# Moving the transposed layer input inside SBUF: six distances from a 128-byte boundary, one for each sub-layer

## The chip, the cores and the metric

The kernel runs on one core of a Trainium2 chip. The core has a matrix engine (TensorE, PE in the tables; its weight loads stand in a row of their own, PEld), a vector engine (VectorE, DVE), an engine for activation functions (ScalarE, ACT), GpSimd (POOL), and SyncE (SP), which here issues the DMAs. SBUF is the on-chip memory with 128 partitions; PSUM takes what TensorE produces. The metric is the device time of one launch in microseconds (us); a lower one is better. Each number of the profile comes from one profiled execution. A word is four bytes, the size of one float32.

## The reference

The computation is a decoder trunk of two layers on an input of 256 positions by 1024 features. Each layer has three sub-layers, and each sub-layer begins by normalising its input:

```python
for l in range(DEPTH):                      # DEPTH = 2
    h = h + 0.5 * swiglu(rms_norm(h, ffn1_norm[l]), ffn1_w_in[l], ffn1_w_out[l])
    u = rms_norm(h, mix_norm[l])
    ... = jnp.split(u @ w_in[l], split_points, axis=-1)      # nine parts
    y_s = mamba2_branch(...)                # SSD branch, 2048 wide
    y_d = deltanet_branch(...)              # gated delta rule, 8 heads
    merged = (sigmoid(gate_s) * (y_s @ ssm_w_branch[l])
              + sigmoid(gate_d) * (y_d @ dn_w_branch[l]))
    h = h + merged @ w_out[l]
    h = h + 0.5 * swiglu(rms_norm(h, ffn2_norm[l]), ffn2_w_in[l], ffn2_w_out[l])
return rms_norm(h, final_norm)
```

`swiglu` multiplies by a 1024 x 5632 matrix, forms silu(gate) * up, and multiplies by a 2816 x 1024 matrix. The mixer's `w_in` has 1024 rows and 11,312 columns.

## The kernel before

Every large matrix product is made in split precision. A float32 operand `a` is written as a high part and a low part, both of the type float32r, and the product is the sum of three matmuls: high by high, high by low, low by high (`mm3`, `mm3w`). The weights come from DRAM in tiles of 128 x 1024 (`wraw`, L95), and ScalarE and VectorE split each into `whi` (L60) and `wlo` (L63), some tiles ahead of the matmuls.

A matmul has two operands in SBUF: the stationary one, 128 x 128, which a weight load brings into the array, and the moving one, which streams through it, one column after another. In the profile's rows a matmul of the form `128*128 128x512` has a stationary operand of 128 x 128 and 512 moving columns.

The normalised input of a sub-layer is transposed on TensorE (`hnT`, L184) and split into the two tiles `uTh` and `uTl`. Each has 8 blocks (`KT`) of 256 words in every partition, so 8192 bytes. `rms_chain` writes them (ScalarE the high part, VectorE the low one), and three helpers read them:

- `tok_chunk` has the input as the **stationary** operand and 512 columns of the weights as the moving one (matmuls `f` in the feed-forward sub-layers and `t` in the mixer, L209 to L211).
- `chan_chunk` has 128 columns of the weights as the stationary operand and the 256 positions of the input as the **moving** one (matmuls `fc` in the feed-forward sub-layers, and `kk`, `qq`, `vv`, `zd`, `bc` and `xs` in the mixer, L214 to L216).
- `scalars` in the mixer does the same with 48 columns of weights (`psm`).

The other large products do not read the input: the feed-forward output product (`o`, stationary `gh` and `gl`), the branch products (`b`) and the mixer's output product (`o`, stationary `mh` and `ml`), all with 512 moving columns of the weights, through the same lines L209 to L211.

The order of the sub-layers is `ffn`, `mixer`, `ffn` for each of the two layers. `norm_in` makes the next sub-layer's input and is called once at the start and then by `close`, at the end of every sub-layer but the last: six times in all. Each product of a sub-layer runs in the order in which it is written, for the mixer in the order of the list `ORDER`. The framework places each tile once, at a fixed address, pool by pool and in the order of first use, and rounds a tile up to a multiple of 32 bytes.

In the built program every tile that is an operand of a large matmul starts at a multiple of 128 bytes of its partition, apart from `uTh` and `uTl`: ahead of them lies `mhalf`, one word wide, which takes 32 bytes. So `uTh` is at byte 32,928 and `uTl` at byte 41,120, each 32 bytes or 8 words behind a multiple of 128. The slices that a matmul takes of these tiles are 128 or 256 words apart, so each slice stands at the same distance as its tile.

Of the kernel before, what the change touches and what calls it, by code (L numbers as in the profile page):

```python
# [7 lines left out]
F32 = mybir.dt.float32  # L8
F32R = mybir.dt.float32r
# [7 lines left out]
P = 128  # L17
D = 1024
S = 256
# [3 lines left out]
KT = D // P  # L23
FC = FF // 256
GS = 4
LPW = 48 * 5 + 16 + 1
# [3 lines left out]
NRAW = 5  # L30
NSPL = 5
START = 2

# [10 lines left out]
def trunk_kernel(ctx, tc, x, wst, wsm, norms, lpar, rpar, cst, out):  # L46
    nc = tc.nc
    V, A, G, PE = nc.vector, nc.scalar, nc.gpsimd, nc.tensor

    cpool = ctx.enter_context(tc.tile_pool(name="cpool", bufs=1))  # L50
# [3 lines left out]
    sm = ctx.enter_context(tc.tile_pool(name="sm", bufs=1))  # L54
# [4 lines left out]
    def act(o, i, func=AF.Copy, **kw):  # L59
        return A.activation(out=o, in_=i, func=func, **kw)  # L60
# [4 lines left out]
    def stt(o, a, s, b, op0, op1):  # L65
        return V.scalar_tensor_tensor(out=o, in0=a, scalar=s, in1=b, op0=op0, op1=op1)
# [6 lines left out]
    def f(ap):  # L73
        return ap.bitcast(F32)

    def tmp2(name):
        return s2.tile([P, 512], F32, tag="s2", name=name)

    def trb(name):
        return trp.tile([P, 512], F32, tag="tr", name=name)  # L80
# [25 lines left out]
    def ahead(key, n, fn):  # L106
        while state[key] < min(n, n_halves):
            fn(state[key])
            state[key] += 1

    def take():
        j = state["taken"]
        state["taken"] = j + 1
        ahead("loaded", j + NSPL + NRAW - 1, load)
        ahead("prepped", j + 1 if state["hold"] else j + NSPL, prep)
        return halves.pop(j)
# [28 lines left out]
    LIMT = cs[:, 3 * P + 64 : 4 * P]  # L145
    SEL = [cs[:, 4 * P : 5 * P], cs[:, 5 * P : 6 * P]]
    LAST = cs[:, 6 * P : 7 * P]
    mhalf = cpool.tile([P, 1], F32, name="mhalf")
    V.memset(mhalf[:], -0.5)

    one = cpool.tile([1, P], F32, name="one")
# [5 lines left out]
    Y = [cpool.tile([P, 512], F32, name=f"Y{i}") for i in range(2)]  # L157
    for y in Y:
        G.memset(y[:], 0.0)
    uTh = cpool.tile([P, KT, S], F32R, name="uTh")  # L160
    uTl = cpool.tile([P, KT, S], F32R, name="uTl")

    def rstd_of(t):

# [9 lines left out]
    def rms_chain(t, nw):  # L174
        r = rstd_of(t)
        hns = []
        for n in range(2):
            hn = tmp2("hn")
            ins = stt(hn[:], h[:, t, n * 512 : (n + 1) * 512], r, nw[n], ALU.mult, ALU.mult)
            hns.append(hn)  # L180
        for n in range(2):
            bank = trb("hnT")
            for k in range(4):
                PE.transpose(bank[:, k * P : (k + 1) * P], hns[n][:, k * P : (k + 1) * P], ident)  # L184
            oh = uTh[:, 4 * n : 4 * n + 4, t * P : (t + 1) * P]
            ol = uTl[:, 4 * n : 4 * n + 4, t * P : (t + 1) * P]
            bv = bank[:].rearrange("p (k t) -> p k t", k=4)
            done = [act(oh, bv), tt(ol, bv, f(oh), ALU.subtract)]
        return ins, done

    def norm_in(nw, add=None):

        for t in range(2):
            with tc.high_priority(offset=PRI):
                if add:
                    add(t)
                ins, done = rms_chain(t, nw)
            if t == 0:
                state["hold"] = False
                n = state["taken"]  # L200
                if not add:
                    ahead("prepped", n + 1, prep)
                    with tc.issue_after(done[0].ins), tc.issue_after(done[1].ins):
                        ahead("prepped", n + START, prep)
                with tc.issue_after(ins.ins):
                    ahead("prepped", n + 2, prep)
# [10 lines left out]

    def tok_chunk(ps, ks):

        ws = [(k, take()) for k in ks[::2]]  # L220
        for t in range(2):
            for k0, (wh, wl) in ws:
                for k in range(2):
                    kt = k0 + k
                    mm3(
                        ps[t][:],
                        uTh[:, kt, t * P : (t + 1) * P],
                        uTl[:, kt, t * P : (t + 1) * P],
                        wh[:, k * 512 : (k + 1) * 512],
                        wl[:, k * 512 : (k + 1) * 512],  # L230
                        kt == 0,
                        kt == KT - 1,
                    )

    def chan_chunk(ps):

        ws = [take(), take()]
        for a in range(2):
            for q in range(2):
                wh, wl = ws[q]  # L240
                for k in range(4):
                    kt = 4 * q + k
                    c0 = k * 256 + a * P
                    mm3w(
                        ps[:, a * 256 : (a + 1) * 256],
                        wh[:, c0 : c0 + P],
                        wl[:, c0 : c0 + P],
                        uTh[:, kt, :],
                        uTl[:, kt, :],
                        kt == 0,  # L250
                        kt == KT - 1,
                    )
# [76 lines left out]

    def mixer(l, nxt):  # L330
        with tc.issue_after(state["last"].ins):
            lp = cpool.tile([P, LPW], F32, tag="lp", name="lp")
            nc.sync.dma_start(lp[:], lpar[l])
            rp = cpool.tile([P, RPW], F32, tag="rp", name="rp")
            nc.sync.dma_start(rp[:], rpar[l].partition_broadcast(P))
            wsr = s2.tile([P, KT, 48], F32, tag="s2", name="wsr")
            nc.sync.dma_start(wsr[:], wsm[l])
# [50 lines left out]

        def scalars():
            psm = trb("psm")  # L390
            for kt in range(KT):
                mm3w(psm[0:48, 0:S], wsh[:, kt, :], wsl[:, kt, :], uTh[:, kt, :], uTl[:, kt, :], kt == 0, kt == KT - 1)
            smT = s2.tile([48, S], F32, tag="s2", name="smT")
            act(smT[:], psm[0:48, 0:S])
            pst = trb("pst")
            for t in range(2):
                PE.transpose(pst[:, t * 48 : (t + 1) * 48], smT[:, t * P : (t + 1) * P], ident[0:48, 0:48])
            pv = pst[:, 0:96].rearrange("p (t c) -> p t c", t=2)
            scr = s2.tile([P, 5, 2, 40], F32, tag="s2", name="scr")
            xb, ax, z, s_, q_ = (scr[:, i] for i in range(5))  # L400
            tt(xb, pv[:, :, 0:40], rp[:, None, 0:40].to_broadcast([P, 2, 40]), ALU.add)
            act(dq[:, :, 8:16], pv[:, :, 40:48], AF.Tanh, scale=0.5)
            ts(dq[:, :, 8:16], dq[:, :, 8:16], 0.5, ALU.mult, 0.5, ALU.add)
            ea = small([P, 40], "ea", 1)
            act(ea[:], alog, AF.Exp)
            stt(ax, xb, -1.0, xb, ALU.mult, ALU.max)
            act(z, ax, AF.Exp, scale=-1.0)
            ts(s_, z, 2.0, ALU.add)
            V.reciprocal(out=s_, in_=s_)
            tt(s_, s_, z, ALU.mult)  # L410
            tt(q_, s_, s_, ALU.mult)
            ts(z, q_, 1.0 / 15.0, ALU.mult)
            for d_ in (13.0, 11.0, 9.0, 7.0, 5.0, 3.0):
                stt(z, z, 1.0 / d_, q_, ALU.add, ALU.mult)
            stt(z, z, 1.0, s_, ALU.add, ALU.mult)
            ts(ax, xb, 0.0, ALU.max)
            stt(sp[:], z, 2.0, ax, ALU.mult, ALU.add)
            stt(la[:], sp[:], -1.0, ea[:, None, :].to_broadcast([P, 2, 40]), ALU.mult, ALU.mult)
            yield
            psr = trb("psr")  # L420
            for t in range(2):
                PE.matmul(psr[0:40, t * 256 : (t + 1) * 256], la[:, t, :], UU, start=True, stop=True)
            pr = psr[:].rearrange("p (t c) -> p t c", t=2)
            V.tensor_copy(rows[0:32], pr[0:32, :, 0:P])
            V.tensor_copy(rows[32:40], pr[32:40, :, P : 2 * P])
            nc.sync.dma_start(rdram[:], rows[:].rearrange("p t c -> p (t c)"))
            pac = trb("pac")
            for t in range(2):
                PE.transpose(pac[:, t * 40 : (t + 1) * 40], rows[:, t, :], ident[0:40, 0:40])
            V.tensor_copy(ac[:], pac[:, 0:80].rearrange("p (t c) -> p t c", t=2))  # L430
            V.tensor_copy(dq[:, :, 0:8], ac[:, :, 32:40])
            yield
            psp = trb("psp")
            for c in range(4):
                PE.matmul(psp[:, c * 16 : (c + 1) * 16], SEL[c % 2], dq[:, c // 2, :], start=True, stop=True)
            for a in range(2):
                V.tensor_copy(
                    pq[64 * a : 64 * a + 64].rearrange("p k h c -> p c k h"),
                    psp[64 * a : 64 * a + 64, 0:64].rearrange("p (c k h a) -> p c k h a", c=4, k=2, h=4)[:, :, :, :, a],
                )  # L440
# [709 lines left out]
```

## Time and profile before

| | before |
|---|---|
| median of 3 runs | 1592.82 us (1592.76 to 1594.43) |
| the profiled execution, its own time | 1593.43 us |
| its span, from the first to the last instruction | 1591.6 us |
| TensorE busy | 1572.3 us, 99% of the span |
| VectorE busy | 1069.1 us, 67% |
| ScalarE busy | 880.1 us, 55% |
| granted TensorE clock | 0.999 of full speed |

Of each group of instructions the profile gives the busy time, which is the union of their spans, and the mean span of one. Matmuls are pipelined: one starts while the one before it is still in the array, so the mean span of a matmul is longer than the distance from its start to the next one's start. That distance is called the pitch here. It sets how long a run of matmuls takes, and it is read from the timeline, which gives the start of each instruction in us: the first start, the last start, and the number of steps between them.

### The profile page before, as it was taken

The page shows a single profiled execution, that of the slowest core. Times are in us where ns is not written, and L with a number is a line of the kernel's source. Part 1 is how long each engine was busy: PE and PEld are TensorE (multiplying, and loading weights), DVE is VectorE, ACT ScalarE, POOL GpSimd, SP SyncE. Part 2 cuts the span into 40 slices and gives each one's busy share as a digit, 9 for nine tenths or more (in the row PEclk, how much of TensorE's full clock was granted, in tenths as well). Part 3 has the DMA queues.
Part 4 walks back from the last instruction along what each step waited for, and adds up shares of the span by engine and source line. Part 5 has one row for each costly group of instructions (what it writes and reads, how often), then busy time and mean ns, then how long its engine had stood idle before and what let it go on. Part 6 is the DMA issues. An engine that isn't in the chain of part 4 may idle for free.

```text
span 1591.6 us, 28859 instructions
## 1 busy us (share of the span) xinstructions
PE 1572.3 (99%) x11672; PEld 1420.9 (89%) x11672; DVE 1069.1 (67%) x1550; ACT 880.1 (55%) x1416; POOL 58.1 (4%) x60
## 2 busy tenths in 40 slices
PE   8999999999999999999999999999999999999998
PEld 7999879999888888999899987899998888889986
DVE  5555468957899766555465555698579996675554
ACT  5444468756565654444354444686656665454443
POOL 0000020000000000000000001000000000000000
PEclk9999999999999999999999999999999999999999
DMA  7555465543465456555565565655436555555562
GB/s 268 193 188 195 161 203 192 166 149 117 173 214 172 159 170 189 188 192 190 173 207 190 186 196 174 197 176 180 129 120 207 178 170 175 172 175 194 187 196 96
DMA packets 91915, 284.73 MB, mean 179 GB/s; under 512 B 22069, under 2 KB 23045, under 8 KB 90758
## 3 DMA queue, kind: packets, MB, share of 16 engines
q1 hardware_dynamic: 91782, 282.90, 54.8%
q8 instruction: 91, 1.49, 0.4%
q14 instruction: 42, 0.34, 0.1%
HBM read 280.94 MB, written 1.92 MB: 178 GB/s over the span
## 4 chain that ended last, share of the span: by engine, by line
PE 91%; DVE 4%; DMA 2%; ACT 1%; POOL 1%; issue 0%; SPq 0%; POOLq 0%; ACTq 0%
PE fc L216 9%; PE fc L214 9%; PE fc L215 9%; PE o L211 6%; PE o L209 5%; PE o L210 5%; PE t L209 4%; PE t L210 3%; PE t L211 3%; PE b L211 3%; PE b L210 2%; PE b L209 2%; PE xs L215 2%; PE xs L214 2%; PE xs L216 2%; DVE wlo L63 1%
## 5 line engine op out<-in xcount | busy, mean ns | idle before, releaser
L63 DVE TENSOR_TENSOR wlo<-wraw,whi 128x1024 fp32r<-128x1024 f32 x504 | 613.6, 1223 | 376.4 <-ACT whi L60 369.3
L60 ACT ACTIVATE whi<-wraw 128x1024 fp32r<-128x1024 f32 x504 | 531.0, 1060 | 429.3 <-PE fc L215 176.2
L214 PE MATMUL fc<-uTh,whi 128*128 128x256 f32 x1280 | 357.4, 279 | 0.0
L215 PE MATMUL fc<-uTl,whi 128*128 128x256 f32 x1280 | 357.0, 279 | 0.0
L216 PE MATMUL fc<-uTh,wlo 128*128 128x256 f32 x1280 | 357.0, 279 | 0.0
L215 PEld LDWEIGHTS fc<-uTl,whi 128*128 128x128 f32 x1280 | 240.6, 188 | 0.2
L214 PEld LDWEIGHTS fc<-uTh,whi 128*128 128x128 f32 x1280 | 240.6, 188 | 0.2
L216 PEld LDWEIGHTS fc<-uTh,wlo 128*128 128x128 f32 x1280 | 240.6, 188 | 0.0
L209 PE MATMUL o<-whi,gh 128*128 128x512 f32 x352 | 137.3, 390 | 0.0
L210 PE MATMUL o<-wlo,gh 128*128 128x512 f32 x352 | 137.3, 390 | 0.0
L211 PE MATMUL o<-whi,gl 128*128 128x512 f32 x352 | 137.0, 389 | 0.0
L209 PE MATMUL t<-whi,uTh 128*128 128x512 f32 x256 | 103.2, 404 | 1.0 <-ACT uTh L60 1.0
L210 PE MATMUL t<-wlo,uTh 128*128 128x512 f32 x256 | 101.6, 397 | 0.0
L211 PE MATMUL t<-whi,uTl 128*128 128x512 f32 x256 | 101.1, 396 | 0.0
L211 PEld LDWEIGHTS o<-whi,gl 128*128 128x128 f32 x352 | 66.1, 188 | 13.8
L210 PEld LDWEIGHTS o<-wlo,gh 128*128 128x128 f32 x352 | 66.1, 188 | 13.6
L209 PEld LDWEIGHTS o<-whi,gh 128*128 128x128 f32 x352 | 66.1, 188 | 13.4
L209 PE MATMUL b<-whi,bh 128*128 128x512 f32 x192 | 76.3, 399 | 0.0
L210 PE MATMUL b<-wlo,bh 128*128 128x512 f32 x192 | 74.9, 390 | 0.0
L211 PE MATMUL b<-whi,bl 128*128 128x512 f32 x192 | 74.3, 394 | 0.6 <-DVE bl L63 0.6
L214 PE MATMUL xs<-uTh,whi 128*128 128x256 f32 x256 | 73.1, 286 | 0.0
L216 PE MATMUL xs<-uTh,wlo 128*128 128x256 f32 x256 | 71.6, 280 | 0.0
(259 smaller groups left out, 2915.6 us busy)
## 6 DMA issues: line engine op xcount, KB each, us to landing
wraw<-in_wst_dram SPq DMA_DIRECT2D x504, 512.0 KB, 4.3
dc<-rdram SPq DMA_DIRECT2D x8, 1024.0 KB, 9.2
nw<-in_norms_dram SPq DMA_DIRECT2D x6, 512.0 KB, 4.9
gb<-rdram SPq DMA_DIRECT2D x8, 256.0 KB, 6.1
h<-in_x_dram SPq DMA_DIRECT2D x4, 256.0 KB, 3.1
out_dram<-fo SPq DMA_DIRECT2D x4, 256.0 KB, 2.3
dq<-X SPq DMA_DIRECT2D x2, 256.0 KB, 4.8
cs<-in_cst_dram SPq DMA_DIRECT2D x1, 384.0 KB, 8.2
```

The source lines that it names most:

```text
L60: return A.activation(out=o, in_=i, func=func, **kw)
L63: return V.tensor_tensor(out=o, in0=a, in1=b, op=op)
L209: PE.matmul(ps, lh, rh, start=start, stop=False)
L210: PE.matmul(ps, lh, rl, start=False, stop=False)
L211: PE.matmul(ps, ll, rh, start=False, stop=stop)
L214: PE.matmul(ps, wh, mh, start=start, stop=False)
L215: PE.matmul(ps, wh, ml, start=False, stop=False)
L216: PE.matmul(ps, wl, mh, start=False, stop=stop)
```

## The change

The two tiles of the input become 32 words longer, and start at a multiple of 128 bytes. Each sub-layer uses a view of them that begins some words behind the start: the feed-forward sub-layer that opens layer 0 uses 16, the mixer 24, the second feed-forward sub-layer 4; in layer 1 the three use 12, 20 and 28.

For the start at a multiple of 128 bytes, `mhalf` moves to another pool (`sm`), and so that the tiles behind the input keep their place relative to 128 bytes, the tile `lp` is padded from 257 to 272 words; the DMA still writes 257. In the built program `uTh` is now at byte 32,896 and `uTl` at byte 41,216; the tiles behind `lp` all lie 256 bytes further on, and so at the same distance from a multiple of 128 as before, up to the pool `sm` at the end, whose small tiles move by 288 bytes, or 8 words relative to 128 bytes. The tiles `Y`, `nw`, `lp` and `one` move from 8 words to 0. The instructions of every engine, their order and their waits are the same in both programs.

```diff
+PLACES = (16, 24, 4, 12, 20, 28)
...
-    mhalf = cpool.tile([P, 1], F32, name="mhalf")
+    mhalf = sm.tile([P, 1], F32, name="mhalf", bufs=1)
...
-    uTh = cpool.tile([P, KT, S], F32R, name="uTh")
-    uTl = cpool.tile([P, KT, S], F32R, name="uTl")
+    uT = [cpool.tile([P, KT * S + 32], F32R, name=name) for name in ("uTh", "uTl")]
+    place = {"n": 0}
+
+    def input_at(w):
+
+        return [u[:, w : w + KT * S].rearrange("p (k t) -> p k t", k=KT) for u in uT]
...
-            oh = uTh[:, 4 * n : 4 * n + 4, t * P : (t + 1) * P]
-            ol = uTl[:, 4 * n : 4 * n + 4, t * P : (t + 1) * P]
+            oh, ol = (u[:, 4 * n : 4 * n + 4, t * P : (t + 1) * P] for u in place["u"])
...
     def norm_in(nw, add=None):
 
+        place["u"] = input_at(PLACES[place["n"]])
+        place["n"] += 1
...
     def tok_chunk(ps, ks):
 
+        uTh, uTl = place["u"]
...
     def chan_chunk(ps):
 
+        uTh, uTl = place["u"]
...
-            lp = cpool.tile([P, LPW], F32, tag="lp", name="lp")
-            nc.sync.dma_start(lp[:], lpar[l])
+            lp = cpool.tile([P, 272], F32, tag="lp", name="lp")
+            nc.sync.dma_start(lp[:, 0:LPW], lpar[l])
...
         def scalars():
             psm = trb("psm")
+            uTh, uTl = place["u"]
```

## The prediction

> **What bounds the kernel now.** I read the page first: the engines' busy time, the granted clock, the chain that ended last.
>
> ```profile
> span 1591.6 us, 28859 instructions
> PE 1572.3 (99%) x11672; PEld 1420.9 (89%) x11672; DVE 1069.1 (67%) x1550; ACT 880.1 (55%) x1416; POOL 58.1 (4%) x60
> ...
> PEclk9999999999999999999999999999999999999999
> ...
> PE 91%; DVE 4%; DMA 2%; ACT 1%; POOL 1%; issue 0%; SPq 0%; POOLq 0%; ACTq 0%
> ```
>
> TensorE is busy for 1572.3 of 1591.6 us at the full clock, and 91% of the chain is its own. It has no time in which to wait, so the only thing that a move of its operands can alter is how fast it runs. A busy PE does not say how fast: for that I take the groups by shape, and then the pitch from the timeline. The groups that read the input, and the one that does the same work without it (`o`), are these:
>
> ```profile
> L214 PE MATMUL fc<-uTh,whi 128*128 128x256 f32 x1280 | 357.4, 279 | 0.0
> L215 PE MATMUL fc<-uTl,whi 128*128 128x256 f32 x1280 | 357.0, 279 | 0.0
> L216 PE MATMUL fc<-uTh,wlo 128*128 128x256 f32 x1280 | 357.0, 279 | 0.0
> L209 PE MATMUL o<-whi,gh 128*128 128x512 f32 x352 | 137.3, 390 | 0.0
> ...
> L209 PE MATMUL t<-whi,uTh 128*128 128x512 f32 x256 | 103.2, 404 | 1.0 <-ACT uTh L60 1.0
> L210 PE MATMUL t<-wlo,uTh 128*128 128x512 f32 x256 | 101.6, 397 | 0.0
> L211 PE MATMUL t<-whi,uTl 128*128 128x512 f32 x256 | 101.1, 396 | 0.0
> ...
> L214 PE MATMUL xs<-uTh,whi 128*128 128x256 f32 x256 | 73.1, 286 | 0.0
> ...
> L215 PE MATMUL bc<-uTl,whi 128*128 128x256 f32 x128 | 36.7, 286 | 0.0
> ...
> L216 PE MATMUL qq<-uTh,wlo 128*128 128x256 f32 x128 | 35.7, 279 | 0.0
> L209 PE MATMUL f<-whi,uTh 128*128 128x512 f32 x64 | 26.5, 416 | 1.3 <-ACT uTh L60 1.3
> ...
> L214 PE MATMUL psm<-uTh,wsh 128*48 128x256 f32 x16 | 4.5, 279 | 0.0
> ```
>
> The input is the moving operand of `fc` (3 x 1280), of `xs` (three rows of 256), of `bc`, `zd`, `qq`, `vv` and `kk` (15 rows of 128, the first and the last shown) and of `psm` (three rows of 16): 3840 + 768 + 1920 + 48 = 6576 matmuls of 256 columns. It is the stationary operand of `t` (768) and `f` (three rows of 64, 192): 960 matmuls of 512 columns. The rows already show a difference: `t` and `o` are the same product, yet one `t` takes 396 to 404 ns and one `o` 390.
>
> The timeline gives the pitches. First `fc`, with the input moving at 8 words behind 128 bytes and the weights at 0:
>
> ```profile
> 59.78 0.28 PE L214 MATMUL fc<-uTh,whi 128*128 128x256 f32 x1
> ...
> 64.22 0.28 PE L216 MATMUL fc<-uTh,wlo 128*128 128x256 f32 x1
> ```
>
> 38 steps in 4.44 us, 116.8 ns each. Then `o`, where both operands are at 0:
>
> ```profile
> 159.98 0.39 PE L209 MATMUL o<-whi,gh 128*128 128x512 f32 x1
> ...
> 165.42 0.39 PE L209 MATMUL o<-whi,gh 128*128 128x512 f32 x1
> ```
>
> 24 steps in 5.44 us, 226.7 ns. Last `t`, with the weights moving at 0 and the stationary input at 8 words:
>
> ```profile
> 448.01 0.40 PE L209 MATMUL t<-whi,uTh 128*128 128x512 f32 x1
> ...
> 458.51 0.40 PE L209 MATMUL t<-whi,uTh 128*128 128x512 f32 x1
> ```
>
> 45 steps in 10.50 us, 233.3 ns. No wait lies inside the three stretches. So **8 words of distance go with 6.6 ns more per matmul of 512 columns** (233.3 less 226.7). Per column, `fc` (116.8 for 256, 233.6 for 512) runs at the pace of `t`, and not at the pace of `o`.
>
> **The change part by part.** No instruction, wait or DMA is added, taken away or moved on any queue; what changes are addresses. By distance: each of the four feed-forward sub-layers has 3840 / 4 = 960 moving and 192 / 4 = 48 stationary uses, each of the two mixers (768 + 1920 + 48) / 2 = 1368 and 768 / 2 = 384.
>
> *Distances 4, 12, 20 and 28* (three feed-forward sub-layers and one mixer) are odd multiples of 4 words. Moving: 3 x 960 + 1368 = 4248. Stationary: 3 x 48 + 384 = 528. In the trace of before the operands of these matmuls stand at multiples of 8 words, so no row shows such a distance. Bounds for one moving use: below, the pace without any loss that distance brings; the nearest row is half an `o`, 113.4 ns, a gain of 3.4 ns; a further one is what the second 256 columns of `o` cost over `fc`, 226.7 - 116.8 = 109.9 ns, a gain of 6.9 ns. Above, the whole 6.6 ns of the step from `o` to `t` on each matmul. I take +3.3 ns, which is that step scaled from 512 to 256 columns: the new positions are a finer misplacement than the one that costs 6.6 ns per 512, and I price it as one more such step. 4248 x 3.3 ns = 14.0 us. For a stationary use I take one more step of 6.6 ns, with bounds of -6.6 (the pace of `o`) and +13.2: 528 x 6.6 ns = 3.5 us.
>
> *Distances 16 and 24* (one feed-forward sub-layer, one mixer) are multiples of 8, as before: 2328 moving and 432 stationary uses. I take nothing. The bounds are the same: -3.4 ns (or -6.9) and +6.6 per moving use, -6.6 and +6.6 per stationary one.
>
> The rule that speaks against this sum is in the Trainium skill, "SBUF — State Buffer", section "Specifications (TRN2)": SBUF has lines of 16 bytes, and what costs is a crossing to a new line. All six distances, 0 and 8 too, are multiples of 16 bytes, so by that rule none needs an extra line, and the time would not change. The step from `o` to `t` is between two such distances and measures 6.6 ns, so the trace shows a dependence that the rule does not give.
>
> *What lies beside.* The path of TensorE has little slack for the sum to disappear in. In the six stretches in which the input is read:
>
> ```profile
> 25.00:137.50 112.50, 112.50 (x966) 112.46 (x965) 62.70 (x71) 54.08 (x70) 0.00 (x0) 1.00 0.61 195
> 199.10:589.00 389.90, 386.94 (x3139) 344.61 (x3138) 307.54 (x523) 249.01 (x464) 23.80 (x21) 1.00 0.53 172
> 626.60:739.00 112.40, 112.40 (x965) 112.40 (x964) 62.60 (x71) 54.05 (x70) 0.00 (x0) 1.00 0.60 195
> 813.10:925.50 112.40, 112.40 (x965) 112.40 (x964) 62.61 (x71) 54.05 (x70) 0.00 (x0) 1.00 0.59 195
> 987.10:1375.00 387.90, 386.87 (x3140) 344.58 (x3139) 307.61 (x524) 248.78 (x464) 23.80 (x21) 1.00 0.54 173
> 1412.50:1525.00 112.50, 112.50 (x966) 112.50 (x965) 62.72 (x71) 54.05 (x70) 0.00 (x0) 1.00 0.61 195
> ```
>
> The columns are the window's length and then busy time and count of PE, PEld, DVE, ACT and POOL, the clock, and the share and GB/s of the DMAs. In the feed-forward stretches PE is busy throughout and VectorE for 62.7 of 112.5 us: a slower TensorE lengthens them by its whole loss, and a faster one is not held up. In the mixers PE is idle for 3.0 and 1.0 us, so at most that much of a loss could be hidden; VectorE at 307.5 of 389.9 us could hold a gain back.
>
> *The writes of the input* move too:
>
> ```profile
> L60 ACT ACTIVATE uTh<-hnT 128x512 fp32r<-128x512 f32 x24 | 14.0, 595 | 13.2 <-PE hnT L184 12.0
> ...
> L63 DVE TENSOR_TENSOR uTl<-hnT,uTh 128x512 fp32r<-128x512 f32 x24 | 15.7, 686 | 5.8 <-ACT uTh L60 5.7
> ...
> lp<-in_lpar_dram SPq DMA_DIRECT2D x2, 128.5 KB, 6.0
> ```
>
> 24 of each, mostly behind the matmuls of the product that is ending. I cost them at nothing; uncovered, a tenth more on both kinds would be 3.0 us, with as much for a gain. `mhalf` in another pool and the padded `lp` (two loads of the same bytes, ahead of their use) cost nothing; if the loads were uncovered and a tenth longer it would be 1.2 us.
>
> Sum: 14.0 + 3.5 = 17.5 us on the profiled execution's own 1593.43 us, 1610.9. The median before is 0.6 us lower, so I predict 1610.
>
> The Trainium skill ("TensorE: Matmul & The Clock Gate", section "Step-by-step: what each phase is for") says that weight loads have an SBUF read port of their own and take nothing from the running matmul. By that the stationary distance is free and the sum is 14.0 us; `t` against `o`, where only the stationary input's distance differs, disagrees by 6.6 ns.
>
> **The rivals.** *No effect of these distances.* The fast pace of `o` could be special to 0, with every other distance at the common pace of `t` and `fc`. For it: both run at one pace per column though one has the input stationary and the other moving. Then only noise is left, 1593. The Trainium skill's rule of 16-byte lines (the section named above) ends at the same time.
>
> *Faster.* At some distances the moving stream and the weight load could fall into step as they do in `o`. If only 16 and 24, the coarser ones, do: 2328 x 3.4 + 432 x 6.6 ns = 10.8 us, 1582. If all six do: 6576 x 3.4 + 960 x 6.6 ns = 28.7 us, 1564. For it: `o` does get 226.7 ns. Against it: `fc` already has one operand at 0 and does not reach that pace. It decides as soon as its gain on 2328 uses exceeds the loss on 4248, that is, if the odd distances lose under 10.8 us / 4248 = 2.5 ns per moving use and nothing on the stationary side.
>
> *Dearer.* The odd distances could cost the full 6.6 ns per moving use: 4248 x 6.6 + 528 x 6.6 ns = 31.5 us, 1625; with 16 and 24 like them, 6576 x 6.6 + 960 x 6.6 ns = 49.7 us, 1643. For it: a loss may fall on each matmul, whatever its columns. Against it: `fc` and `t` agree per column.
>
> **How the numbers follow.** Chances: the forecast 0.40, with its own range from 1600 to 1618 (half of the moving price, and one and a half times it); dearer 0.15; no effect 0.17; faster at 16 and 24 0.18, at all six 0.10. The range from 1582 to 1640 leaves out the gain at all six and the top of the dearer case. Within 0.2% (3.2 us, about what can be told from no change) is the case of no effect, 0.17; faster 0.28; slower 0.55.
>
> **What would show it.** The stretches can be laid side by side, since the order is the same. Right: `fc` at 116.8 ns in the first feed-forward sub-layer (16) and near 120 in the other three (4, 12, 28), so 112.5 us there and about 115.7 after; the mixer of layer 0 (24) as before, that of layer 1 (20) about 7 us longer, with `t` near 240 ns. Wrong: pitches that differ among 4, 12, 20 and 28 as much as between them and 16, or an `fc` below 116. `o` must stay at 226.7 everywhere; if it moves, something other than the distance has changed.

## The result

| | before | changed |
|---|---|---|
| median, 4 runs each | 1593.62 us (1592.76 to 1594.56) | 1600.93 us (1600.20 to 1605.15) |
| ratio changed to before, of the means | | 1.0051, 95% interval 1.0032 to 1.0070 |
| the profiled execution, its own time | 1593.43 us | 1605.15 us |
| its span | 1591.6 us | 1603.3 us |
| its granted TensorE clock | 0.999 of full speed | 0.998 |

The change costs 7.3 us of the medians (8.2 us of the means). The changed kernel's profiled execution is the slowest of its four, 4.2 us above their median; the account below says where its extra time lies. The page of the changed kernel:

```profile
span 1603.3 us, 28859 instructions
...
PE 1579.5 (99%) x11672; PEld 1429.6 (89%) x11672; DVE 1069.7 (67%) x1550; ACT 881.7 (55%) x1416; POOL 57.9 (4%) x60
```

The count of instructions is the same, and so are VectorE's and ScalarE's busy times within 2 us; TensorE is busy 7.2 us longer.

To read the pitch of a whole sub-layer in one row I use the view of busy time by window, for the tile `fc` alone. Each row is one feed-forward sub-layer, 90 us long, in which TensorE runs one `fc` after the other. A matmul lasts 0.28 us, so 2.4 of those counted were already running when the window opened: the pitch is 90.00 us / (count - 2.4). Before:

```profile
40.00:130.00 90.00, 90.00 (x773) 90.00 (x773) 6.69 (x16) 5.87 (x16) 1.00 0.59 190
640.00:730.00 90.00, 90.00 (x774) 90.00 (x773) 6.62 (x16) 5.86 (x16) 1.00 0.58 188
830.00:920.00 90.00, 90.00 (x774) 90.00 (x773) 6.61 (x16) 5.86 (x16) 1.00 0.57 188
1430.00:1520.00 90.00, 90.00 (x774) 90.00 (x773) 6.62 (x16) 5.86 (x16) 1.00 0.58 188
```

773 or 774 in each, 116.7 ns. The changed kernel, with 16, 4, 12 and 28 words:

```profile
40.00:130.00 90.00, 90.00 (x772) 90.00 (x771) 6.63 (x16) 5.85 (x16) 1.00 0.57 188
645.00:735.00 90.00, 90.00 (x767) 90.00 (x766) 6.64 (x16) 5.63 (x16) 1.00 0.57 188
835.00:925.00 90.00, 90.00 (x767) 90.00 (x766) 6.64 (x16) 5.88 (x16) 1.00 0.57 186
1440.00:1530.00 90.00, 90.00 (x766) 90.00 (x765) 6.63 (x16) 5.84 (x16) 1.00 0.56 186
```

772 at 16 words, 767, 767 and 766 at the odd multiples of 4. The pitches in the rest of this text are the mean distance from one start to the next over all matmuls of the kind in a sub-layer, without the few gaps above 150 ns (260 for 512 columns). By that measure these four are 117.07, 117.78, 117.78 and 117.77 ns, against 116.68 before in all four.

The mixers, from the timeline. The longest stretch of 256-column matmuls without a break, in the first mixer before:

```profile
241.13 0.28 PE L215 MATMUL kk<-uTl,whi 128*128 128x256 f32 x1
...
268.90 0.28 PE L216 MATMUL kk<-uTh,wlo 128*128 128x256 f32 x1
```

238 steps in 27.77 us, 116.7 ns. The same stretch in the changed kernel, at 24 words and then at 20, and a stretch of `t` in each mixer:

```profile
241.53 0.28 PE L221 MATMUL kk<-uTl,whi 128*128 128x256 f32 x1
...
269.74 0.28 PE L222 MATMUL kk<-uTh,wlo 128*128 128x256 f32 x1
...
452.94 0.39 PE L215 MATMUL t<-whi,uTh 128*128 128x512 f32 x1
...
463.91 0.39 PE L217 MATMUL t<-whi,uTl 128*128 128x512 f32 x1
...
1035.76 0.28 PE L221 MATMUL kk<-uTl,whi 128*128 128x256 f32 x1
...
1063.79 0.28 PE L222 MATMUL kk<-uTh,wlo 128*128 128x256 f32 x1
...
1244.58 0.39 PE L215 MATMUL t<-whi,uTh 128*128 128x512 f32 x1
...
1255.49 0.39 PE L217 MATMUL t<-whi,uTl 128*128 128x512 f32 x1
```

238 steps in 28.21 us (118.5 ns) at 24 words, and in 28.03 us (117.8) at 20. 47 steps of `t` in 10.97 us (233.4 ns) and in 10.91 us (232.1). Over all of a mixer the 256-column pitch is 118.47 at 24 words and 117.89 at 20, where the kernel before had 116.81 and 116.85; `t` is 232.7 and 232.1, where it had 233.2.

So where the time went, as count by difference in pitch: the four feed-forward sub-layers 960 x (0.39 + 1.10 + 1.10 + 1.09) ns = 3.5 us, the mixers 1344 x (1.66 + 1.04) ns = 3.6 us, the stationary uses a gain of 1.0 us. That is 6.1 us of the 11.7 by which the two spans differ. The other 5.6 us are mostly pauses of TensorE in the mixers. Waits of TensorE before:

```profile
PE hnT L184 <- DVE hn L66: 4.3, 8, 1.1
...
PE cbb L778 <- DVE vb L63: 2.0, 2, 1.6
```

and after:

```profile
PE cbb L787 <- DVE vb L64: 6.1, 2, 3.3
PE hnT L189 <- DVE hn L67: 4.9, 9, 1.3
```

The wait at the end of the recurrence (`cbb`) is 4.1 us longer in this execution. The sum of its waits is 6.1 us there against 2.0, and 3.5 in the kernel of the first experiment and 3.7 in a faster one below, so it does not follow the pitch, and its length here is at least in part that of this execution. The medians differ by 7.3 us, nearer to the 6.1 of the pitches.

### The profile page after: what moved, and what is told of

Read it like the earlier page. It is cut to its first block, busy times and chain, and to the rows that moved or that the text cites. A ratio compares the mean times of both kernels' runs of the same rounds, so it can differ in the third digit from the quotient of the medians.

```text
span 1603.3 us, 28859 instructions
## 1 busy us (share of the span) xinstructions
PE 1579.5 (99%) x11672; PEld 1429.6 (89%) x11672; DVE 1069.7 (67%) x1550; ACT 881.7 (55%) x1416; POOL 57.9 (4%) x60
## 4 chain that ended last, share of the span: by engine, by line
PE 91%; DVE 4%; DMA 2%; ACT 2%; POOL 1%; issue 0%; SPq 0%; POOLq 0%; ACTq 0%
PE fc L220 9%; PE fc L221 9%; PE fc L222 9%; PE o L217 5%; PE o L215 5%; PE o L216 5%; PE t L215 4%; PE t L217 3%; PE t L216 3%; PE b L217 3%; PE b L216 2%; PE b L215 2%; PE xs L220 2%; PE xs L221 2%; PE xs L222 2%; DMA dc<-rdram 1%
```

## The experiments

Theory A is the prediction's: the distance behind a multiple of 128 bytes sets the pitch. Its first rival, B, is that other addresses that moved do it. "Place" below is the distance of the high part in words; the "room" is what lies between the end of the high part and the start of the low part. The kernel before had place 8 and no room; the changed kernel has 32 words of room, because each tile became 32 words longer.

### The same distance as before in the changed layout, and other distances in it

`e1_all8`, against the changed kernel:

```diff
-PLACES = (16, 24, 4, 12, 20, 28)
+PLACES = (8, 8, 8, 8, 8, 8)
```

> The changed layout (longer tiles, mhalf and lp moved) with all six sub-layers at 8 words, the distance of before. Theory A, the distance alone sets the pitch: fc 116.7 ns, the mixer's 256-column matmuls 116.8, t 233.2, and the time of before, 1593.6 us within 2. Rival B, the other moved addresses cost it (uTl 128 bytes further from uTh, the tiles behind 256 bytes further on, the small tiles by 8 words): the pitches of the changed kernel, 117.1 to 118.5 ns, and about 1601 us.

Measured: 1605.04 us against 1596.38 for the kernel before on the same chip, ratio 1.0058 (1.0042 to 1.0073). In the view by window, tile `fc`:

```profile
40.00:130.00 90.00, 90.00 (x767) 90.00 (x766) 6.63 (x16) 5.80 (x16) 1.00 0.58 186
645.00:735.00 90.00, 90.00 (x762) 90.00 (x761) 6.65 (x16) 5.84 (x16) 1.00 0.57 185
835.00:925.00 90.00, 90.00 (x762) 90.00 (x761) 6.63 (x16) 5.85 (x16) 1.00 0.59 186
```

767 and then 762 where the kernel before had 774: 117.8 and 118.5 ns, the mixers 118.3, `t` 232.1 to 232.4. The high part is at the very byte at which it was before, and the pitch is another. Theory A falls: one of the other addresses matters. The first sub-layer and the later ones differ by 0.7 ns at one and the same place, which no run explains.

`e2_all0`, the same with `PLACES = (0, 0, 0, 0, 0, 0)`:

> All six at 0 words, a multiple of 128 bytes, like every other operand of a large matmul. Theory A1, both operands at 0 is what gives o its 226.7 ns: t goes to 226.7 and fc to about half, 113.4 ns, so 28.7 us less than before, about 1565 us. Rival A2, the fast pace of o needs a stationary operand at 0 but the moving 256 columns keep a common pace: t 226.7, fc 116.7, about 1587 us. Rival A3, a moving operand at 0 loses as at 16, 24 and the odd distances: fc 117.1 to 118.5 ns and 1590 to 1600 us.

Measured: 1601.6 us against 1596.38, ratio 1.0026 (1.0013 to 1.0039). `fc` is 117.78 ns in all four, the mixers 117.8, `t` 231.4. A1 and A2 fall; A3 gave the range of the pitch, not its reason. The time is above its range, in a comparison in which the kernel before was slower too.

`e3_swap`, the same with `PLACES = (24, 16, 20, 0, 4, 8)`:

> The six sub-layers at 24, 16, 20, 0, 4 and 8 words: the mixers get what feed-forward sub-layers had and the other way round. Theory A, the pitch belongs to the distance: fc 118.5 ns in the first (24), 117.8 to 117.9 in the third (20), 116.7 in the last (8); the mixers' 256-column matmuls 117.1 (16) and 117.8 (4). Rival C, the mixers are slower in themselves at any distance but 8: the mixers 117.9 to 118.5 ns again, and the feed-forward sub-layers 117.1 to 117.8.

Measured (one run, 1605.25 us): `fc` 118.5 ns at 24, 117.8 at 20 and at 0; the mixers 117.7 at 16 and 117.85 at 4. 24 words are slow in either kind of sub-layer, so rival C falls. Theory A misses twice more: the last, 8 words, is at 118.5 and not at 116.7, and 16 words have 117.7 in the mixer where the first sub-layer of the changed kernel had 117.1.

`e4_fine`, the same with `PLACES = (1, 6, 2, 3, 7, 5)`:

> The six sub-layers at 1, 6, 2, 3, 7 and 5 words, no multiple of 4 among them. Theory D, memory is fetched in pieces of 4 words (16 bytes), and a matmul that starts inside a piece needs one more: a step above the 117.8 ns of distance 4 in every sub-layer, of 1.7 to 3.3 ns (4 words of 256 columns at 109.9 ns are 1.7), so fc 119.5 to 121 ns and some 1610 to 1620 us. Theory E, pieces of 8 words: the same as 4 words, fc about 117.8 ns and 1600 us. Rival F, no pieces, the pitch drifts with the distance: fc between 116.7 and 117.8 ns.

Measured (one run, 1613.17 us): 122.2 ns at 1, 121.5 at 2, 117.5 at 3, 120.0 at 5; in the mixers 120.9 at 6 and 117.65 at 7. None of the three theories holds: 3 and 7 cost no more than 4, 1 costs 4.4 ns more. The time lies in theory D's range, but not for D's reason: a rule by pieces of 16 bytes would have made all six dearer than 4 words.

### The room between the two parts, and the place of what lies behind

Both kernels put the two parts in one tile, with a place and a room for each sub-layer. `f1_gap`:

```diff
-    uT = [cpool.tile([P, KT * S + 32], F32R, name=name) for name in ("uTh", "uTl")]
+    uT = cpool.tile([P, WORDS], F32R, name="uT")
...
-        return [u[:, w : w + KT * S].rearrange("p (k t) -> p k t", k=KT) for u in uT]
+        return [uT[:, i : i + KT * S].rearrange("p (k t) -> p k t", k=KT) for i in (w[0], w[0] + KT * S + w[1])]
...
+PLACES = ((8, 0), (8, 0), (8, 32), (8, 64), (8, 32), (0, 0))
+WORDS = 4224
```

> Both parts of the input in one tile, with the distance of the high part and the room between the parts chosen for each sub-layer; the weights stay as many bytes behind a multiple of 512 as before. In the order of the sub-layers, high part at 8, 8, 8, 8, 8, 0 words, and the low part 8192 bytes further on plus 0, 0, 128, 256, 128, 0 bytes. Before it was 8 and 0. Theory B1, the 128 bytes more between the two parts cost: fc 116.7 ns in the first sub-layer, the first mixer 116.8; the third (128 bytes) 118.5 and the second mixer 118.3 as in the run with all at 8. Theory B2, the shift of the weights by 256 bytes costs: fc 116.7 ns and the mixers 116.8 in all with 8 words. Under A, the distance alone, already fallen for 8 words: fc 118.5 ns. For the last, 0 words with 0 bytes between, A says 117.8 ns again.

`f2_gap_far` has `WORDS = 4288`, and everything behind the input 256 bytes further on:

> The same six places of the input, with the weights and everything behind the input 256 bytes further on than in the kernel with the same places (the place of the weights in the changed kernel). Theory B1 (room between the two parts): the same pitches as there, 116.7 ns in the first sub-layer and 118.5 in the third. Theory B2 (shift of the weights by 256 bytes): 118.5 ns in both, and in the mixers 118.3.

One run each, 1604.21 and 1599.91 us, with 1599.41 in a single run of the kernel before. The view by window of `f1_gap`, tile `fc`: 8 words without room, with 32 words of room, with 64, and 0 words without room:

```profile
40.00:130.00 90.00, 90.00 (x774) 90.00 (x773) 6.74 (x17) 5.87 (x16) 1.00 0.59 188
645.00:735.00 90.00, 90.00 (x767) 90.00 (x766) 6.62 (x16) 5.86 (x16) 1.00 0.59 187
835.00:925.00 90.00, 90.00 (x773) 90.00 (x773) 6.62 (x16) 5.87 (x16) 1.00 0.59 188
1440.00:1530.00 90.00, 90.00 (x752) 90.00 (x751) 6.62 (x16) 5.46 (x15) 1.00 0.58 187
```

774, 767, 773 and 752. The second of these sub-layers in `f2_gap_far`:

```profile
645.00:735.00 90.00, 90.00 (x762) 90.00 (x761) 6.61 (x16) 5.63 (x16) 1.00 0.59 187
```

With no room the pitch of before is back, 116.67 ns, and so it is with 64 words (116.68); 32 words cost 1.1 ns in `f1_gap` and 1.8 in `f2_gap_far` (118.5), the same two values that `e1_all8` had in different sub-layers of one kernel. In every other sub-layer the two agree, `fc` with 116.68, 116.68 and 119.99, so 256 bytes more between the input and the weights change nothing without room. B1 holds and B2 falls. The surprise is the last row: at 0 words with no room `fc` takes 120.0 ns in nearly every step, 3.3 more than at 8, while the stationary `f` drops to 227.8, the pace of `o`. With 32 words of room the same place had 117.78 (`e2_all0`). Theory A's value for it falls again.

`h3_gaps` asks for other rooms: `PLACES = ((8, 8), (8, 64), (8, 16), (8, 24), (0, 64), (8, 48))`, `WORDS = 4224`.

> The weights at 0 again. The high part at 8, 8, 8, 8, 0 and 8 words; between the parts 8192 bytes plus 8, 64, 16, 24, 64 and 48 words. Theory P, the room between the parts counts by its remainder to 64 words (256 bytes): the mixers (64 words) as with none, 116.8 ns at 8 words and 120.0 at 0. The others are open; if any room that is no multiple of 64 words costs as 32 did, fc is 117.8 to 118.5 ns in all four feed-forward sub-layers; if the room only puts the low part at another distance, fc lies between the pitches of the two distances.

Measured (one run, 1601.74 us): `fc` 117.8 ns with 8, 16 and 24 words of room, 118.5 with 48; the mixers with 64 words of room 116.8 at place 8 and 119.9 at place 0, as with none. Theory P holds: the room counts by its remainder to 256 bytes. Any other room that was tried costs 1.1 to 1.8 ns at place 8. That the room only puts the low part at another place does not hold for all of them: 32 and 48 words put it at 40 and 56, whose pitches without room are 117.4 and 118.3 (table at the end), and `fc` lies above both ends with 117.8 to 118.5 and 118.5.

### The changed kernel's distances without the room

`h1_near`: `PLACES = ((16, 0), (24, 0), (4, 0), (12, 0), (20, 0), (28, 0))`, `WORDS = 4224`.

> The six distances of the changed kernel, 16, 24, 4, 12, 20 and 28 words, with the two parts of the input 8192 bytes apart as before, not 8320. Theory G, the 128 bytes more between the parts are the whole loss: fc 116.7 ns and the mixers 116.8 at all six, the time of before within 3 us. Rival H, the distance matters too when the parts are 8192 bytes apart, as 0 words did (120.0 ns): pitches that leave 116.7 by 0.5 to 3.3 ns at some of the six, and a time that follows from them, up to 22 us over before if all were at 120.

Measured: 1602.7 us against 1594.9, ratio 1.0050 (1.0036 to 1.0064), the same loss as with the room. But its parts are others. In the view by window, tile `fc`, at 16, 4, 12 and 28 words:

```profile
40.00:130.00 90.00, 90.00 (x766) 90.00 (x766) 6.38 (x16) 5.83 (x16) 1.00 0.58 186
645.00:735.00 90.00, 90.00 (x774) 90.00 (x773) 6.84 (x17) 5.88 (x16) 1.00 0.60 188
835.00:925.00 90.00, 90.00 (x763) 90.00 (x762) 6.61 (x16) 5.86 (x16) 1.00 0.59 185
1440.00:1530.00 90.00, 90.00 (x796) 90.00 (x795) 6.64 (x16) 5.98 (x17) 1.00 0.61 194
```

766, 774, 763 and 796: 117.8, 116.8, 118.3 and **113.5 ns**. The mixers are at 119.9 (24) and 119.1 (20). Summed over the counts, the feed-forward sub-layers gain 0.4 us and the mixers lose 1344 x (3.11 + 2.24) ns = 7.2 us. Theory G falls, rival H holds: without the room the distance matters more, not less, and at 28 words it is a gain.

`h4_fine_near` tries further places: `PLACES = ((32, 0), (1, 0), (2, 0), (40, 0), (3, 0), (6, 0))`.

> Parts 8192 bytes apart, at 32, 1, 2, 40, 3 and 6 words. Theory Q, the place counts by its remainder to 32 words: fc 120.0 ns at 32 as at 0, and 116.7 at 40 as at 8. Rival T, by its remainder to 64 words: other values at 32 and 40. At 1, 2, 3 and 6 words: with pieces of 4 words a matmul that starts inside one needs one more, and its pitch is above that of 0 or 4 words by 1.7 to 3.3 ns; without pieces it is not above 120.0.

Measured (one run, 1607.80 us): `fc` 118.7 ns at 32, 117.65 at 2, 117.4 at 40, 120.0 at 6; the mixers 123.2 at 1 and 117.5 at 3. Theory Q falls and T holds: 32 is not like 0 (120.0) and 40 not like 8 (116.7), so the period is not 128 bytes, on which the change is built. Again 3 words cost little and 1 word the most, so no theory of pieces is borne out.

### The weights moved instead of the input

`h2_weights8` moves every tile behind `rp` by 8 words, the weights among them:

```diff
-            rp = cpool.tile([P, RPW], F32, tag="rp", name="rp")
-            nc.sync.dma_start(rp[:], rpar[l].partition_broadcast(P))
+            rp = cpool.tile([P, RPW + 8], F32, tag="rp", name="rp")
+            nc.sync.dma_start(rp[:, 0:RPW], rpar[l].partition_broadcast(P))
...
+PLACES = ((8, 0), (8, 0), (16, 0), (0, 0), (16, 0), (8, 32))
+WORDS = 4224
```

> The weights, and all tiles of large operands behind them, moved by 8 words (32 bytes), so gh and the weights are both at 8 in o. The input, parts 8192 bytes apart: 8, 8, 16, 0, 16 words, and in the last sub-layer 8 with 128 bytes more between the parts. Theory R, what counts is the place of the input relative to the weights: at 8 words fc 120.0 ns and f 227.8 (as 0 had with the weights at 0), at 16 words fc 116.7, f and t 233; o unchanged at 226.8. Rival S, the input's own place behind 128 or 256 bytes counts: fc 116.7 ns at 8 and 120.0 at 0 words as before, t 233 at 8, and o would leave 226.8.

One run, 1603.61 us. The view by window, tile `fc`, at 8, 16, 0 words, and 8 with room:

```profile
40.00:130.00 90.00, 90.00 (x752) 90.00 (x752) 6.20 (x15) 5.50 (x16) 1.00 0.57 185
645.00:735.00 90.00, 90.00 (x774) 90.00 (x773) 6.57 (x16) 6.08 (x17) 1.00 0.59 188
835.00:925.00 90.00, 90.00 (x762) 90.00 (x762) 6.61 (x16) 5.80 (x16) 1.00 0.58 185
1440.00:1530.00 90.00, 90.00 (x767) 90.00 (x766) 6.61 (x16) 5.84 (x16) 1.00 0.59 188
```

752 at 8 words, 774 at 16: 119.99 and 116.68 ns, the two values that 0 and 8 words had with the weights at 0. `f` follows, 227.85 at 8 words; `t` is 227.7 at 8 and 233.2 at 16. `o`, whose two operands moved together, stays at 226.8. Theory R holds in each of these, S falls: **the place of the input relative to the weights sets the pitch**. In `fc` the weights are only the stationary operand, and the input lies at the byte at which it was in `f1_gap`; so the pitch of the moving stream depends on where the stationary operand lies. The writing of the weights, which moved with them, is not the reason: in the steps in which neither VectorE nor ScalarE runs, 132 and 141 of the first sub-layer's, `fc` has 116.7 ns in `f1_gap` and 120.0 in `h2_weights8`. (The tile that the DMA writes moved too; in `w1_low8`, below, it keeps its place, and the pitch changes all the same.) The Trainium skill ("TensorE: Matmul & The Clock Gate", section "Step-by-step: what each phase is for") gives the two operands read ports of their own and says that loading the next weights takes no read bandwidth from the running matmul. Here the place of the weights is worth 3.3 ns of each matmul, and the measurement decides.

`w1_low8` moves the low weights alone, by 8 words, against `f1_gap`:

```diff
-        lo = wpool.tile([P, 1024], F32R, tag="wlo", name="wlo", bufs=NSPL)
+        lo = wpool.tile([P, 1024 + 64], F32R, tag="wlo", name="wlo", bufs=NSPL)[:, 8:1032]
...
+PLACES = ((8, 0), (8, 0), (28, 0), (48, 0), (28, 0), (0, 0))
+WORDS = 4160
```

> Only the low parts of the weights lie 8 words further, the high parts at 0; the input's parts 8192 bytes apart, at 8, 8, 28, 48, 28 and 0 words. In fc the weights are stationary alone: L221 (high by low input) runs while the low weights of L222 are loaded, the other two while high weights are. Theory W, a matmul's pitch is set by its moving operand's place against the weights that are loaded beside it: only L221 of each three sees another place, so the mean leaves 116.7, 113.5 and 113.4 by about a third of the step that all three make when all weights move (at 8 words 3.3 ns, so 117.8). Rival X, the weights of a matmul itself: L222 changes instead, with the same mean. Rival Y, the weights do not count and the run with all of them moved had another reason: fc 116.7 at 8, 113.5 at 28, 113.4 at 48, 120.0 at 0 words as before.

Measured (one run, 1609.91 us): `fc` 117.74 ns at 8, 117.8 at 28, 118.85 at 48, 118.3 at 0; the mixers 117.7 and 117.8. Rival Y falls. The third of the step that W and X both give is met at 8 words (117.7) alone. By the table at the end the thirds at 28, 48 and 0 words are +1.9, +1.3 and -0.6 ns; measured are +4.3, +5.5 and -1.7. W and X are not told apart: at 28 words all three matmuls of a group leave the 113 to 114 ns that they had, for 116.9, 117.9 and 118.7, so a change in one of them moves the others too. `o`, which streams high and low weights in turn past a stationary operand that did not move, rises from 226.8 to between 231.7 and 233.3. So the pace of a sequence depends on the places of all its operands. It is not simply fast where the weights agree: at 0 words it was slower with both parts of them in line (120.0).

### A version that is faster than both

`b1_all28`: `PLACES = ((28, 0),) * 6`, `WORDS = 4224`.

> All six sub-layers at 28 words, the two parts 8192 bytes apart. Theory R, the place of the input relative to the weights sets the pitch, whatever the sub-layer: fc 113.5 ns in all four feed-forward sub-layers as in the one that had 28 words, 4 x 960 x 3.2 ns = 12.3 us less; the mixers' 2736 matmuls of 256 columns at 113.5 too, 9.0 us less; together about 21 us less than before, some 1574 us. Rival U, 113.5 ns came from that one sub-layer's start or from its place at the end: the others at 116.7 to 120 ns and a time of 1590 to 1605 us. Between the two, the mixers keep 117 to 120 ns and only the feed-forward part gains: 1580 to 1590 us.

Measured: 1579.00 us against 1596.14 for the kernel before on the same chip, ratio 0.9898 (0.9880 to 0.9915). The view by window, tile `fc`:

```profile
40.00:130.00 90.00, 90.00 (x796) 90.00 (x796) 6.61 (x16) 6.12 (x17) 1.00 0.61 195
630.00:720.00 90.00, 90.00 (x796) 90.00 (x795) 6.61 (x16) 5.79 (x16) 1.00 0.61 195
820.00:910.00 90.00, 90.00 (x796) 90.00 (x795) 6.61 (x16) 6.05 (x17) 1.00 0.61 194
1420.00:1510.00 90.00, 90.00 (x797) 90.00 (x796) 7.02 (x17) 5.79 (x16) 1.00 0.61 196
```

796 or 797 in every row: 113.5 ns, half of an `o`. The mixers are at 114.1, `t` still at 233.4. 960 x 4 x 3.2 ns + 1344 x 2 x 2.75 ns = 19.7 us; 17.1 arrive. In the profiled executions TensorE is busy 19.0 us less (1553.3 us) and idle 4.3 us more. Theory R holds, U falls.

`s1_scan` looks for other places: `PLACES = ((36, 0), (52, 0), (44, 0), (60, 0), (60, 0), (48, 0))`.

> Parts 8192 bytes apart, at 36, 52, 44, 60, 60 and 48 words. By theory T, remainders to 64 words (256 bytes) count, these are six new places. If the place relative to the weights counts by its size alone, on either side alike, 36 words (28 less than 64) gives fc 113.5 ns, 60 gives 116.8 as 4, 52 and 44 give 118.3 and 119.1 as 12 and 20, 48 gives 117.8 as 16. If not, the pitches lie anywhere from 113.4 to 120 ns, and a place as good as 28 is one with a locked pattern of 113 and 114.

Measured (one run, 1601.76 us): `fc` 118.7 ns at 36, 119.25 at 44, 117.15 at 60, **113.4 at 48**; the mixers 119.1 at 52 and 117.2 at 60. The place does not count by its size alone: 36 is far from 28 and 48 far from 16. At 48 `f` is 229.5, 3.8 ns less than at 28, and at 60 `f` and `t` are at 227.5 and 228.0, as fast as at 0.

`b2_all48`: `PLACES = ((48, 0),) * 6`, `WORDS = 4224`.

> All six sub-layers at 48 words, parts 8192 bytes apart. Theory R, the place relative to the weights sets both pitches: fc 113.4 ns, the mixers' 256-column matmuls near 114, and t near 229.5 as f had at 48, where 28 words had 233.4. Against the kernel with all at 28, 960 x 3.7 ns = 3.6 us less, about 1575.5 us. Rival V, the stationary pitch does not follow the place in the mixers: t at 233 and 1579 us.

Measured: 1577.64 us against 1596.00, ratio 0.9889 (0.9873 to 0.9906). `fc` is 113.4 to 113.6 ns and `t` 229.2, so theory R holds for the stationary uses too; but the mixers' 256-column matmuls are at 115.3, 1.2 above those at 28. The two versions' intervals overlap.

## Why the prediction was wrong

The direction was right and the size was not: +17.5 us were forecast (1610), +7.3 measured (1600.93), under half. The time lies inside the range from 1582 to 1640, and at the lower end of the forecast's own range from 1600 to 1618; half of the moving price, which that end is said to be, gives 1603. The direction was luck in part: of the 7.1 us that the moving uses lose, 2.6 are at 16 and 24 words, priced at nothing, and all of them were measured with a room between the two parts that the sum does not have.

1. *What bounds the kernel* was right. TensorE's pitch is what the change moved: of 11.7 us between the spans, 6.1 are pitches, and most of the rest is a wait whose length differs between kernels without following the pitch. The writes of the input, `mhalf` and `lp` cost nothing that a row shows. `o` stays at 226.7 to 226.9 ns in every feed-forward sub-layer of the changed kernel.

2. *"Distances 4, 12, 20 and 28"* is the step that failed: the term for the moving uses. It took the 6.6 ns from `o` to `t`, scaled to +3.3 ns for a moving use, and 14.0 us. Measured: +1.0 to +1.1 ns in each, 4.6 us. The 6.6 ns were no price of a misplaced line which a finer misplacement pays again. They were the difference between two places of the input relative to the weights (`t` at place 0 has 227.7 ns, at place 8 233.2), and say nothing of a third place. That `fc` came out alike at 4, 12 and 28, as the prediction asked, is owed to the room: without it these places have 116.8, 118.3 and 113.5 ns.

3. The stationary uses at these distances were given +6.6 ns and 3.5 us; they measure -3.1 to +0.2 ns. Here the sign failed, and with 16 and 24 the stationary uses gain 1.0 us. The kernel before already stood at one of the dearest places, 233.2 ns; 234.1 is the highest seen in a mixer.

4. *"Distances 16 and 24"* were given nothing because they are multiples of 8 words. At 24 the mixer pays 1.66 ns, 2.2 us, the dearest of the six.

5. The premise of all three, that the distance behind 128 bytes is the variable, fell. The period is 256 bytes (`h4_fine_near` rules out 128; `h3_gaps` and `f2_gap_far` find 256), the reference is the weights (`h2_weights8`), and the second variable, the room of 128 bytes that the longer tiles put between the two parts, is not in the sum at all. At 8 words the layout with it costs 8.7 us of the medians (`e1_all8`), and the changes in pitch there come to 9.3 us. In this change it evens things out: with it, the six distances cost 0.4 to 1.7 ns; without it (`h1_near`), from -3.2 to +3.1.

6. Of the rivals, *faster* described a gain that exists, and priced it rightly at half of an `o`: 113.4 ns was forecast for it and 113.5 is what 28 words give. It named 16 and 24, or all six, as the places, and the places are 28 and 48, with no room. Its reason, that the streams fall into step, is not shown: regular steps occur at slow places too (last section). *No effect* falls. The Trainium skill ("SBUF — State Buffer", section "Specifications (TRN2)") gives SBUF lines of 16 bytes and a penalty for each crossing to a new line. That rule does not give what was seen here: places that are all multiples of 16 bytes run from 113.4 to 120.0 ns. *Dearer* was not seen at a multiple of 4 words.

What stays open: which weight load a matmul meets (`w1_low8` did not decide), how the places 28 and 48 come out best, and why one place with one room can have two pitches (117.8 and 118.5 ns at 8 words with 32 of room). No rule that was tried gives the order of the places.

## What to carry to other kernels

Where TensorE is the bound, read the pitch of each group of matmuls from the starts in the timeline and compare groups of one shape: `fc` at 116.7 ns where half of an `o` is 113.4 was the trace of a placement that cost 1% of this kernel; `t` at 233 where `o` has 227 showed that the place counts, but `t` kept its 233 ns in the faster kernel with 28 words. Then try places for the operand, all of them over 256 bytes, and keep what is compared at one place to the byte: a tile that grows by 128 bytes moves its neighbour, and that alone was worth as much here as the whole change. Several places can be tried in one run, one for each sub-layer, if each has its own stretch in the trace.

## What the runs showed of the hardware

Pitch of 256-column float32r matmuls by the place of the moving input relative to the weights, both parts 8192 bytes apart, in ns; (m) is measured in a mixer, the others on `fc`:

| place, words | 0 | 1 | 2 | 3 | 4 | 6 | 8 | 12 | 16 | 20 | 24 |
|---|---|---|---|---|---|---|---|---|---|---|---|
| pitch | 120.0 | 123.2 (m) | 117.65 | 117.5 (m) | 116.8 | 120.0 | 116.7 | 118.3 | 117.8 | 119.1 (m) | 119.9 (m) |

| place, words | 28 | 32 | 36 | 40 | 44 | 48 | 52 | 56 | 60 |
|---|---|---|---|---|---|---|---|---|---|
| pitch | 113.5 | 118.7 | 118.7 | 117.4 | 119.25 | 113.4 | 119.1 (m) | 118.3 | 117.2 |

The one at 56 is 0 words with the weights at 8. Three things were not expected. The pitch of the moving stream depends on where it lies relative to the stationary weights, from 113.4 to 123.2 ns. The best place for the input as the moving operand is not the best one for it as the stationary operand: at 0 `fc` is among the slowest (120.0 ns) and `f` and `t` among the fastest (227.8). And a regular step is no sign of a fast place. At 28 words `fc` steps by 113 or 114 ns in 935 of 959 steps, as `o` has 226 or 227; but at 0 words it steps by 120 ns in 948 of 959 (`f1_gap`), and `t` at 28 words by 233 or 234 in nine of ten. The kernel before has one mean, 116.7, with steps of 116 or 117 in over 920 of 959 in three feed-forward sub-layers and with steps from 113 to 120 in the first. At 8 words with the room steps of 116 to 123 follow one another, and the mean depends on the sub-layer (117.8 in the first, 118.5 in the others).
